# Second half of the attention: order of casts, scores and MLP steps, and a residual added by DMA

## The chip, the cores and the metric

The kernel runs on one core of a Trainium2 chip. The metric is the device time of one execution in microseconds (us). Every time in this document is of that one core; the profile shows TensorE as PE (matmuls) and PEld (weight loads), VectorE as DVE, ScalarE as ACT, GpSimd as POOL, and SyncE, which only issues DMAs here, as SP.

## The reference, cut to what matters

A two-layer trunk on 1024 tokens of width 1024, in float32. Layer 0 mixes with a matrix memory, layer 1 with causal attention over a shared low-rank key and value; each mixer is followed by an MLP with squared ReLU. The change lies in layer 1:

```
def causal_mla_attention(q_nope, q_rope, k_nope, k_rope, v):    # 8 heads, blocks of 128 queries
    s = (einsum('bqhd,bkhd->bhqk', qn_b, k_nope)
         + einsum('bqhd,bkd->bhqk', qr_b, k_rope)).astype(float32) * scale
    s = where(kpos[None, :] <= qpos[:, None], s, -inf)
    p = softmax(s, axis=-1)
    return einsum('bhqk,bkhd->bqhd', p.astype(v.dtype), v)

# layer 1
y = mla_mixer(h, ...)                          # attention, then @ w_out
x = x + g1[:, None, :] * rmsnorm(y, norm_g[l, 1])          # "the residual" of this document
h = modulate(rmsnorm(x, norm_g[l, 2]), sh2, sc2)
y = square(relu(h @ w1)) @ w2
x = x + g2[:, None, :] * rmsnorm(y, norm_g[l, 3])
```

## The kernel before, in words

The tokens are worked on in two halves of 512. A float32 product is made of three matmuls on a high and a low part of each operand (`mm3`, L280 to L282), so every weight and every activation is split first: a cast on ACT makes the high part, a subtraction on DVE the low part (`wsplit`, L238 and L239, for weights; `split_mod`, L501 and L502, for activations).

Two streams of work are woven by hand in `two_streams`. The *other* stream is what has to go on in order: here `mixer1` of the second half, that is its key and query latents, its attention (`attention_second`, `attend_beside`), the output projection `wout` and `post`. The *dense* stream is an MLP: here layer 1's MLP on the first half (`sweep1`), whose products need nothing from the second half. The other stream yields numbers. A number is how many dense steps are put into TensorE's order at that place; a 0 forgets what was still due. In `sweep1` each step consists of two pieces that count a half, and each piece is 12 matmuls of 512 columns: a hidden step (`first`: TensorE writes `ps`) or an up step (`up_rows`: TensorE writes `pm` and DVE adds it to the sums, L247). "align" runs the dense stream on until a hidden step is next. The order of TensorE's instructions is thereby written out; on the other engines a scheduler orders what is ready by priority. Work inside `prompt` has high priority: the weight loads with their splits, the softmax, and the evacuations. `tc.issue_after(i)` puts what is issued in its block behind instruction `i` on `i`'s engine; `paced()` uses it to put parts of `residual` and `post` behind the last DVE instruction of the dense piece before. An MLP weight is loaded and split two steps ahead of its products (`AHEAD`). `sweep1` has 64 pieces; behind them comes `sweep2`, the same MLP on the second half, and it needs what `post` makes.

`attend_beside` goes through 16 units: 8 heads, each with 256 queries `j` = 2 (6 key blocks) and then 256 queries `j` = 3 (8 key blocks). A unit has two scores `e` = 0, 1 of 128 queries each; a score is up to 1024 columns wide. `softmax_two` takes it from PSUM: maximum (DVE L1824), two exponentials (ACT L1826), sum and reciprocal (DVE L1829, L1830), two scalings (DVE L1832). For `e` = 0 the probabilities lie in a tile `raw`, shared with the weight loads, for `e` = 1 in two tiles `tmc`. `turned` transposes four blocks on TensorE (L2031) and splits them; `products` multiplies the values with blocks turned two rounds before. Per unit, in TensorE's order: for each pair of key blocks its transposes, then products, and in the first two rounds behind these a score of the *next* unit (`then`); at the unit's end `yield next(dense)`.

`post` calls `residual`: the sum of squares of `y` is made on ACT (L484) and DVE (L488), TensorE sums it over the partitions (L492), a short chain gives the factor, eight DVE instructions scale `y` (L956), eight add the old `x` (L959) that SP has loaded from `xs` (L926), and SP stores each block to `xs` (L962). Then the same begins again on the new `x`: squares, sums, L492. ACT also scales `y` in place (L2701) and DVE makes differences of it (L2702) for the MLP's second half; their results go through L2715 to L2733. `WAITS` are the dense steps put between: ahead of the first sum, after the first and second four blocks, ahead of the second sum.

The lines that set these numbers:

```
        yield from attend_beside(hf, units(), cycle((0.5, 0.5, 0)), lambda: load_o(hf))
...
    WAITS = (2, 1, 0.5, 3, 0, 0)
```

Of the kernel before, what the change touches and what calls it, by code (L numbers as in the profile page):

```python
# [9 lines left out]
F32 = mybir.dt.float32  # L10
# [4 lines left out]
ALU = mybir.AluOpType  # L15
AX = mybir.AxisListType

P = 128
D = 1024
S = 1024  # L20
H = 512
# [61 lines left out]
def kernel(  # L83
# [27 lines left out]
    nc = tc.nc  # L111
# [4 lines left out]
    ts = lambda i, n: slice(i * n, (i + 1) * n)  # L116
# [45 lines left out]
    def scratch(shape, name):  # L162
        return dr.tile(shape, F32, tag=name, bufs=1, name=name)
# [62 lines left out]
    class Half:  # L226
        pass

    pace, follow = [None], [False]

    def paced():

        return tc.issue_after(pace[0]) if pace[0] else nullcontext()

    def wsplit(r, n):
        hi = sb.tile([P, 1024], F32R, tag="ws", bufs=WS, name=f"wh_{next(uid)}")
        lo = sb.tile([P, 1024], F32R, tag="ws", bufs=WS, name=f"wl_{next(uid)}")
        nc.scalar.copy(hi[:, :n], r[:, :n])  # L238
        i = nc.vector.tensor_sub(lo[:, :n], r[:, :n], hi[:, :n].bitcast(F32))  # L239
        if follow[0]:  # L240
            pace[0] = i.ins
        return hi, lo
# [169 lines left out]
    SH1, SC1, G1, SH2, SC2, G2 = range(6)  # L412
    adac = lambda l, part: ada[:, l, ts(part, 8)]
# [60 lines left out]
    def rstd_steps(blocks, n):  # L474

        accs = []
        for b in blocks:
            square_to(accs, b)
        yield
        return sums_rstd(accs[0], n, tmc())  # L480
# [439 lines left out]
    xs = scratch([D, S], "xs")  # L920
    xs_blk = lambda k, half: xs[ts(k, P), ts(half, H)]
# [22 lines left out]

    def residual(y, half, B, src, first, each=None, n3=1, n7=1):

        blk = src(half)
        yield 0
        rs = rstd_steps([y[k] for k in range(KD)], D)
        next(rs)  # L950
        yield first
        rstd = last_of(rs)
        yield 0
        for k in range(KD):
            with paced():
                nc.vector.scalar_tensor_tensor(  # L956
                    y[k], y[k], B[:, k : k + 1], rstd, ALU.mult, ALU.mult
                )
                nc.vector.tensor_add(y[k], y[k], blk(k))  # L959
                if each:  # L960
                    each(k)
            nc.sync.dma_start(xs_blk(k, half), y[k])  # L962
            if k % 4 == 3:
                yield n7 if k == KD - 1 else n3

# [854 lines left out]
    def softmax_two(f, pr, n):  # L1820


        m, l, a = small(1), small(1), small(2)
        nc.vector.reduce_max(m, f[:, :n], axis=AX.X, negate=True)  # L1824
        for g, w in ((0, 512), (1, n - 512)):
            nc.scalar.activation(  # L1826
                pr[g][:, :w], f[:, g * 512 : g * 512 + w], AF.Exp, bias=m, accum_out=a[:, g : g + 1]
            )
        nc.vector.tensor_add(l, a[:, 0:1], a[:, 1:2])  # L1829
        nc.vector.reciprocal(l, l)  # L1830
        for g, w in ((0, 512), (1, n - 512)):
            nc.vector.tensor_scalar(pr[g][:, :w], pr[g][:, :w], l, None, ALU.mult)  # L1832

    def softmax(f, pr, n):
        m, l = small(1), small(1)
# [183 lines left out]
    def attend_beside(hf, units, dense, behind):  # L2019

        def turned(u, b):
            t = hdv(F32R)
            pt = pc()
            turns = [(0, b), (1, b), (0, b + 1), (1, b + 1)]
            if b + 2 == u.nk:
                turns.pop(2)
            for m, (i, kb) in enumerate(turns):  # L2030
                nc.tensor.transpose(  # L2031
                    pt[:, ts(m, P)], u.prs[i][kb // 4][:, ts(kb % 4, P)], ident
                )
            w = len(turns) * P
            split_mod(t[:, 0, :w], t[:, 1, :w], pt[:, :w], None)
            return t

        def products(u, b, t):
            if b == 0:
                u.po = ps()[:, :256]  # L2040
            for kb in (b, b + 1):
                last = kb == u.nk - 1
                o = u.po[:, P:] if last else u.po
                at = slice((kb - b) * 256, (kb - b) * 256 + (P if last else 256))
                mm3(o, *u.v[kb], t[:, 0, at], t[:, 1, at], kb == 0, last)
            if b + 2 == u.nk:
                s = ts(u.j % 2, 256)
                if u.hh < 6:
                    o = tmp()[:, :256]
                    nc.scalar.copy(o, u.po)  # L2050
                    nc.sync.dma_start(oT[ts(u.hh, P), ts(u.j, 256)], o)
                else:
                    split_mod(hf.o.hi[u.hh][:, s], hf.o.lo[u.hh][:, s], u.po, None)

        def unit():
            g = next(units, None)
            if g is None:
                return None
            u = Half()
            (u.hh, u.q, u.kn, u.v), u.j = g  # L2060
            u.nk, u.prs = 2 * u.j + 2, []
            return u

        def score(u, e):
            i = 2 * u.j + e
            st = pm()
            score_two(st, hf.kk, u.q, u.kn, i)
            if e:
                pr = [tmc(), tmc()]
            else:  # L2070
                pr = raw()
                pr = [pr[:, 0:512], pr[:, 512:1024]]
            prompt(softmax_two)(st.rearrange("p a b -> p (a b)"), pr, (i + 1) * P)
            u.prs.append(pr)

        yield "align"
        u = unit()
        for e in range(2):
            score(u, e)
        yield 1  # L2080
        behind_, waiting = [behind], []
        while u:
            then = unit()
            for n, b in enumerate(range(0, u.nk, 2)):
                waiting.append((u, b, turned(u, b)))
                yield 0
                if len(waiting) > 2:
                    products(*waiting.pop(0))
                    yield 0
                if n < 2:  # L2090
                    if then:
                        score(then, n)
                        yield 0
                    elif behind_:
                        behind_.pop()()
            yield next(dense)
            u = then
        for w in waiting:
            products(*w)
# [99 lines left out]
    def attention_second(hf):  # L2199
        pairs = [prepare_pair(p_, hf) for p_ in range(4)]  # L2200
        next(pairs[0])
        yield 0
        for p_ in range(4):
            if p_ < 3:
                yield from primed(pairs[p_], pairs[p_ + 1])
            else:

                yield next(pairs[p_])
                first = loaded_head(0)
                yield from pairs[p_]  # L2210

        def units():
            for hh in range(NH):
                h_ = loaded_head(hh) if hh else first
                if hh == 6:
                    last_o(hf)
                for j in range(2, 4):
                    yield h_, j

        yield from attend_beside(hf, units(), cycle((0.5, 0.5, 0)), lambda: load_o(hf))  # L2220

    def primed(g, then):

# [13 lines left out]
    def load_o(hf):  # L2237
        o, half = hf.o, hf.i
        for b in range(3):
            o.hi.t[b], o.lo.t[b] = k4v(F32R), k4v(F32R)  # L2240
            r = raw().rearrange("p (a b) -> p a b", b=512)
            nc.sync.dma_start(
                r, oT[2 * b * P : (2 * b + 2) * P, ts(half, H)].rearrange("(k p) n -> p k n", p=P)
            )
            nc.scalar.copy(o.hi.t[b], r)
            nc.vector.tensor_sub(o.lo.t[b], r, o.hi.t[b].bitcast(F32))
# [225 lines left out]
    m = [pm(), pm()]  # L2472
# [11 lines left out]
    hf, h = hfs[0], Split()  # L2484
# [281 lines left out]
    ms = [Mlp(0, False), Mlp(1, True)]  # L2766
# [138 lines left out]
    def mixer1(hf, z, attention):  # L2905
        att = attention(hf)
        lat = latent(hf, lambda: next(att))
        next(lat)

        yield from to_x(hf, z)  # L2910
        yield from lat
        yield next(att)
        yield "fill"
        yield from att
        y = FH(claim=True)
        last = wout(b_w_out[0], hf.o, lambda m, pt: evac(y[m], pt), ahead=2 - 2 * hf.i)
        if not hf.i:
            next(last)
        yield 1
        yield "align"  # L2920
        for _ in last:
            yield 0
        yield 1
        if hf.i:
            yield from post(hf, y, B2, x_cols, A3, adac(1, SH2), ms[1], WAITS)
        else:
            yield from post_second(hf, y, B2, x_cols, A3, adac(1, SH2))

# [15 lines left out]
        mixer1(hfs[0], z0, attention_first), bg_rest(),  # L2944
    )

    WAITS = (2, 1, 0.5, 3, 0, 0)
    u0, u1, swept = FH(claim=True), Half(), [False]

    def aside():  # L2950
# [57 lines left out]
```

## Time and profile before

| | |
|---|---|
| median of 3 runs | 2339.51 us |
| lowest and highest of them | 2333.42 and 2341.66 us |
| the profiled execution | 2334.96 us |
| its span in the profile | 2333.2 us |
| PE busy | 2253.4 us, 97% |
| DVE busy | 1682.5 us, 72% |
| ACT busy | 1109.4 us, 48% |
| POOL busy | 137.0 us, 6% |

The span is 1.8 us shorter than the time of the same execution, and that execution is 4.6 us under the median. Overlapped matmuls make PE look full where it only follows its order; where PE does wait, the profile names what ended the wait. A row of the timeline gives the start, the duration, the engine, the line, the tile written and the tiles read; in brackets stands how long the engine had been idle and what it was released by. A row of a group gives count, busy time and mean. PEclk is the granted TensorE clock as a share of full speed.

### The profile page before, as it was taken

How to read it: one execution, taken by the hardware profiler on the slowest of the kernel's cores; microseconds unless marked ns; L12 is line 12 of the kernel's file. 1: busy time of each engine (PE TensorE's matmuls, PEld its weight loads, DVE VectorE, ACT ScalarE, POOL GpSimd, SP SyncE). 2: the span in 40 equal slices, each digit the busy share in tenths (PEclk: the TensorE clock that was granted, in tenths of full speed). 3: DMA queues.
4: the chain of work that ended last, by engine and by line, in shares of the span. 5: the costliest groups of instructions: out<-in, count | busy, mean ns of one | idle time of the engine just before them, and what ended most of it. 6: DMA issues, size and time to landing. Idle time of an engine off the chain costs nothing. (4 is left out here: it accounts for less than half of the span.)

```text
span 2333.2 us, 30865 instructions
## 1 busy us (share of the span) xinstructions
PE 2253.4 (97%) x11050; PEld 1861.1 (80%) x11050; DVE 1682.5 (72%) x2733; ACT 1109.4 (48%) x1925; POOL 137.0 (6%) x228
## 2 busy tenths in 40 slices
PE   8999999999999999999999999998897899999998
PEld 6888887888888878788888877787785688888887
DVE  6677767889887877777757678666638876765556
ACT  4365335865344455445445555444434333354433
POOL 1000000011122210000000000000000211100000
PEclk9999999999999999999999999999998899999999
DMA  9544554668999886677668656844335686666421
GB/s 318 190 122 125 162 155 144 212 215 279 341 293 293 283 302 211 217 220 223 226 193 279 226 177 230 288 142 173 115 96 190 197 258 219 212 215 207 161 90 64
DMA packets 400234, 482.01 MB, mean 207 GB/s; under 512 B 28788, under 2 KB 270513, under 8 KB 400081
## 3 DMA queue, kind: packets, MB, share of 16 engines
q1 hardware_dynamic: 381248, 413.87, 55.3%
q0 software_dynamic: 18832, 66.17, 7.7%
q8 instruction: 87, 1.43, 0.2%
q14 instruction: 67, 0.54, 0.1%
HBM read 358.33 MB, written 121.63 MB: 206 GB/s over the span
## 5 line engine op out<-in xcount | busy, mean ns | idle before, releaser
L238 ACT CAST wh<-raw 128x1024 fp32r<-128x1024 f32 (+4 forms) x301 | 305.1, 1015 | 416.7 <-PE ps L281 150.1
L239 DVE TENSOR_TENSOR wl<-raw,wh 128x1024 fp32r<-128x1024 f32 (+4 forms) x301 | 354.8, 1181 | 191.3 <-ACT wh L238 165.6
L280 PE MATMUL ps<-k,wh 128*128 128x512 f32 x1109 | 438.4, 395 | 4.0 <-ACT wh L238 2.4
L281 PE MATMUL ps<-k,wh 128*128 128x512 f32 x1109 | 433.3, 391 | 3.5 <-DVE k L502 3.5
L282 PE MATMUL ps<-k,wl 128*128 128x512 f32 x1109 | 433.1, 391 | 0.0
L280 PEld LDWEIGHTS ps<-k,wh 128*128 128x128 f32 x1109 | 208.5, 188 | 50.8 <-ACT wh L238 3.4
L281 PEld LDWEIGHTS ps<-k,wh 128*128 128x128 f32 x1109 | 208.7, 188 | 47.7 <-DVE k L502 5.1
L282 PEld LDWEIGHTS ps<-k,wl 128*128 128x128 f32 x1109 | 208.7, 188 | 43.8
L247 DVE TENSOR_TENSOR k<-k,pm 128x512 f32<-128x512 f32 (+1 forms) x194 | 156.6, 836 | 70.2 <-PE pm L282 70.0
L280 PE MATMUL pm<-wh,hd 128*128 128x512 f32 x488 | 195.2, 400 | 8.5 <-DVE k L247 7.7
L282 PE MATMUL pm<-wh,hd 128*128 128x512 f32 x488 | 191.8, 393 | 2.2 <-DVE hd L502 2.2
L281 PE MATMUL pm<-wl,hd 128*128 128x512 f32 x488 | 192.0, 393 | 0.0
L280 PEld LDWEIGHTS pm<-wh,hd 128*128 128x128 f32 x488 | 92.9, 190 | 29.8 <-issue 9.1
L282 PEld LDWEIGHTS pm<-wh,hd 128*128 128x128 f32 x488 | 92.6, 190 | 22.5 <-DVE hd L502 2.8
L281 PEld LDWEIGHTS pm<-wl,hd 128*128 128x128 f32 x488 | 92.7, 190 | 20.0 <-issue 1.2
L280 PE MATMUL pm<-hd,wk 128*128 128x512 f32 x256 | 101.7, 397 | 2.3 <-ACT hd L501 2.3
L281 PE MATMUL pm<-hd,wk 128*128 128x512 f32 x256 | 100.5, 393 | 0.3 <-DVE hd L502 0.2
L282 PE MATMUL pm<-hd,wk 128*128 128x512 f32 x256 | 100.2, 391 | 0.0
L281 PE MATMUL pm<-hd,wh 128*128 128x512 f32 x256 | 99.6, 390 | 0.2 <-DVE hd L502 0.2
L282 PE MATMUL pm<-hd,wl 128*128 128x512 f32 x256 | 99.7, 389 | 0.0
L280 PE MATMUL pm<-hd,wh 128*128 128x512 f32 x256 | 99.2, 390 | 0.1
L986 ACT ACTIVATE tmp<-tmp 128x512 f32<-128x512 f32 x80 | 50.4, 630 | 81.3 <-DVE tmp L247 70.3
(495 smaller groups left out, 4751.4 us busy)
## 6 DMA issues: line engine op xcount, KB each, us to landing
raw<-in_mlp_w_dram SPq DMA_DIRECT2D x160, 512.0 KB, 4.7
raw<-in_mlp_w_dram SPq DMA_DIRECT2D x128, 256.0 KB, 4.7
raw<-in_ada_w_dram SPq DMA_DIRECT2D x54, 512.0 KB, 4.6
raw<-in_a_w_in_dram SPq DMA_DIRECT2D x44, 512.0 KB, 3.9
lo<-wl POOLq DMA_DIRECT2D x32, 512.0 KB, 6.4
s<-k POOLq DMA_DIRECT2D x32, 512.0 KB, 4.1
u<-k POOLq DMA_DIRECT2D x32, 512.0 KB, 5.5
raw<-s SPq DMA_DIRECT2D x32, 512.0 KB, 4.7
```

What stands on the lines that cost most here:

```text
L238: nc.scalar.copy(hi[:, :n], r[:, :n])
L239: i = nc.vector.tensor_sub(lo[:, :n], r[:, :n], hi[:, :n].bitcast(F32))
L247: return f(*a, **k)
L280: nc.tensor.matmul(o, lh, rh, start=start, stop=False)
L281: nc.tensor.matmul(o, lh, rl, start=False, stop=False)
L282: pe_last[0] = nc.tensor.matmul(o, ll, rh, start=False, stop=stop)
L986: nc.scalar.activation(s, s, AF.Relu)
```

## The change

Six edits, five of them in the second half's attention and what follows it:

- `softened()`: a weight's cast and subtraction are issued behind the last exponential (ACT) and the last scaling (DVE) of the latest `softmax_two`. The list is emptied in the last unit.
- `turned`: the four transposes go first through the two blocks of `e` = 0, then through those of `e` = 1. Where they are written stays as it was.
- `attend_beside`: the next unit's score stands ahead of the round's transposes and products, where it stood behind them. In the last unit `load_o` moves in the same way.
- `cycle((0.5, 0))` for `cycle((0.5, 0.5, 0))`: a dense piece in each `j` = 2 unit, none in a `j` = 3 unit.
- `residual` without `src` (second half of layer 1): no loads of `xs` and no additions on DVE. Behind every second block POOL issues a DMA that adds 512 KB of `xs` into `y` in SBUF, and SP then stores the two blocks to `xs`.
- `WAITS` from (2, 1, 0.5, 3, 0, 0) to (2.5, 1.5, 1, 4, 0, 0).

```
+    def softened():
+
+        c = ExitStack()
+        for i in soft:
+            c.enter_context(tc.issue_after(i))
+        return c
 
     def wsplit(r, n):
...
-        nc.scalar.copy(hi[:, :n], r[:, :n])
-        i = nc.vector.tensor_sub(lo[:, :n], r[:, :n], hi[:, :n].bitcast(F32))
+        with softened():
+            nc.scalar.copy(hi[:, :n], r[:, :n])
+            i = nc.vector.tensor_sub(lo[:, :n], r[:, :n], hi[:, :n].bitcast(F32))
...
     def residual(y, half, B, src, first, each=None, n3=1, n7=1):
 
-        blk = src(half)
+        blk = src and src(half)
...
-                nc.vector.tensor_add(y[k], y[k], blk(k))
+                if blk:
+                    nc.vector.tensor_add(y[k], y[k], blk(k))
                 if each:
                     each(k)
-            nc.sync.dma_start(xs_blk(k, half), y[k])
+            if blk:
+                nc.sync.dma_start(xs_blk(k, half), y[k])
+            elif k % 2:
+                x = xs[(k - 1) * P : (k + 1) * P, ts(half, H)].rearrange("(k p) n -> p k n", p=P)
+                nc.gpsimd.dma_start(y.t[k // 2], x, accum_op=ALU.add)
+                nc.sync.dma_start(x, y.t[k // 2])
...
     def softmax_two(f, pr, n):
...
-            nc.vector.tensor_scalar(pr[g][:, :w], pr[g][:, :w], l, None, ALU.mult)
+            d = nc.vector.tensor_scalar(pr[g][:, :w], pr[g][:, :w], l, None, ALU.mult)
+        soft[:] = [e.ins, d.ins]
...
-            for m, (i, kb) in enumerate(turns):
+            for m, (i, kb) in sorted(enumerate(turns), key=lambda t: t[1]):
...
             for n, b in enumerate(range(0, u.nk, 2)):
+                if n < 2:
+                    if then:
+                        score(then, n)
+                        yield 0
+                    elif behind_:
+                        soft.clear()
+                        behind_.pop()()
                 waiting.append((u, b, turned(u, b)))
                 yield 0
                 if len(waiting) > 2:
                     products(*waiting.pop(0))
                     yield 0
-                if n < 2:
-                    if then:
-                        score(then, n)
-                        yield 0
-                    elif behind_:
-                        behind_.pop()()
...
-        yield from attend_beside(hf, units(), cycle((0.5, 0.5, 0)), lambda: load_o(hf))
+        yield from attend_beside(hf, units(), cycle((0.5, 0)), lambda: load_o(hf))
...
-            yield from post(hf, y, B2, x_cols, A3, adac(1, SH2), ms[1], WAITS)
+            yield from post(hf, y, B2, None, A3, adac(1, SH2), ms[1], WAITS)
...
-    WAITS = (2, 1, 0.5, 3, 0, 0)
+    WAITS = (2.5, 1.5, 1, 4, 0, 0)
```

More of the change, by code (lines that the diff above doesn't have):

```diff
@@ L227 @@
         pass
-    pace, follow = [None], [False]
+    pace, follow, soft = [None], [False], []
     def paced():
         return tc.issue_after(pace[0]) if pace[0] else nullcontext()
+    def softened():
[3 more added lines that the diff above has]
+        return c
     def wsplit(r, n):
@@ L1825, in softmax_two @@
         for g, w in ((0, 512), (1, n - 512)):
-            nc.scalar.activation(
+            e = nc.scalar.activation(
                 pr[g][:, :w], f[:, g * 512 : g * 512 + w], AF.Exp, bias=m, accum_out=a[:, g : g + 1]
```

## The prediction, made before the changed kernel ran

> **What bounds the kernel now.** I read the page's head, then busy time and granted clock by stretch, then who waits for whom on PE, then the timeline at the waits.
>
> ```profile
> PE 2253.4 (97%) x11050; PEld 1861.1 (80%) x11050; DVE 1682.5 (72%) x2733; ACT 1109.4 (48%) x1925; POOL 137.0 (6%) x228
> ...
> core 0: us, PE busy (x) PEld busy (x) DVE busy (x) ACT busy (x) POOL busy (x), PEclk, DMA share, GB/s
> 1498.00:1680.00 182.00, 160.29 (x990) 138.60 (x989) 119.74 (x237) 88.56 (x213) 1.40 (x4) 0.97 0.42 146
> 1680.00:1751.00 71.00, 71.00 (x321) 58.99 (x320) 27.57 (x34) 27.31 (x38) 1.75 (x5) 1.00 0.37 111
> 1751.00:1850.00 99.00, 74.41 (x285) 57.00 (x284) 86.79 (x132) 41.63 (x65) 10.18 (x10) 0.84 0.55 179
> ```
>
> PE bounds the kernel: it lacks 80 us (2333.2 - 2253.4). Of these, 21.7 us lie in the attention (1498 to 1680) and 24.6 us in what follows the projection (1751 to 1850); between them PE is full. The clock column adds 0.03 x 182 = 5.5 us in the attention. In the last stretch 0.16 x 99 = 16 us looks larger, but much of it falls on idle time.
>
> ```profile
> PE pc L2031 <- DVE tmc L1832: 17.9, 8, 3.2
> PE pc L2031 <- DVE hd L502: 2.2, 2, 1.3
> ...
> PE pc L492 <- DVE tmc L488: 11.2, 1, 11.2
> PE pm L280 <- DVE k L247: 7.7, 2, 7.5
> ```
>
> In the attention PE waits for the scaled probabilities of `e` = 1; after it, for the squares of the second sum, then for DVE to take up an up step. One attention wait in time:
>
> ```profile
> 1641.14 0.48 PE L1818 MATMUL pm<-k,k 128*128 128x512 f32 x1
> 1641.93 1.22 DVE L1824 TENSOR_REDUCE sm<-pm 128x1 f32<-128x1024 f32 x1
> 1644.03 1.05 ACT L238 CAST wh<-raw 128x1024 fp32r<-128x1024 f32 x1 [1.51 <-DMA raw<-in_mlp_w_dram]
> 1644.98 0.68 ACT L1826 ACTIVATE tmc<-pm,sm 128x512 f32<-128x512 f32 x1
> 1645.11 1.22 DVE L239 TENSOR_TENSOR wl<-raw,wh 128x1024 fp32r<-128x1024 f32 x1 [1.50 <-ACT wh L238]
> 1646.25 1.28 DVE L247 TENSOR_TENSOR k<-k,pm 128x512 f32<-128x512 f32 x2
> 1647.45 0.15 DVE L1829 TENSOR_TENSOR sm<-sm 128x1 f32<-128x1 f32 x1
> 1647.83 0.88 DVE L1832 TENSOR_SCALAR tmc<-tmc,sm 128x512 f32<-128x512 f32 x2
> 1648.38 0.33 PE L2031 MATMUL pc<-ident,tmc 128*128 128x128 f32 x1 [2.85 <-DVE tmc L1832]
> ...
> 1652.64 0.43 PE L2031 MATMUL pc<-ident,raw 128*128 128x128 f32 x1
> 1653.87 0.45 PE L1812 MATMUL pm<-k,k 128*128 128x512 f32 x1
> 1655.80 0.27 PE L2031 MATMUL pc<-ident,raw 128*128 128x128 f32 x1
> ```
>
> The score ends at 1641.6, its probabilities at 1648.7: 7.1 us. The maximum is there at 1643.15, yet the exponential starts at 1644.98, behind a weight's cast that stood in ACT's queue waiting for its DMA. The last three rows: a round of transposes and products takes PE 1.2 us, a score of 768 columns 1.9 us.
>
> **The change part by part.**
>
> *Casts behind the softmax.* They leave 1.8 us of this chain (1643.15 to 1644.98) and the cast's DVE half, 1.14 us to the next start. Undisturbed the chain is 1.22 + two exponentials (1644.98 to 1646.43, 1.45) + 0.4 of small ones + 0.88, with 0.3 to start: 4.3 us for 1024 columns, less for fewer. Behind a held cast the splits of other tiles could queue, but its own releasers run just before it on its own queue. The weight waits too; it is needed two dense steps later, with a piece in every second unit that is eight units, half of the attention. If that cover failed PE would wait for cast and subtraction, 2.3 us each.
>
> *Transposes of `e` = 0 first.* Two of 0.11 us slip under each wait: between 0 and 8 x 0.2 us, taken as 0.
>
> *Scores ahead.* Nothing is added; score `e` = 1 comes one round earlier, and the next unit's score `e` = 0 now stands between a unit's end and the transposes that need `e` = 1. *Fewer steps* takes the piece out of the `j` = 3 units.
>
> ```profile
> L280 PE MATMUL pm<-wh,hd 128*128 128x512 f32 x24 | 9.5, 397 | 0.8 <-ACT raw L1826 0.8
> L280 PE MATMUL ps<-k,wh 128*128 128x512 f32 x19 | 7.5, 392 | 0.0
> ...
> 1757.47 0.39 PE L280 MATMUL ps<-k,wh 128*128 128x512 f32 x1
> 1762.91 0.39 PE L280 MATMUL pm<-wh,hd 128*128 128x512 f32 x1
> ```
>
> One of the three matmuls of a product stands four times in a piece: 24 and 19 (one record missing) are 11 pieces, as the cycle gives; two take 5.44 us, so one 2.72. Eight remain. Distance from the end of score `e` = 1 to the transposes that need it: before, 1.2 or 2.4 us of rounds plus 2.7 where there is a piece. After, for a 1024-column score (begun in a `j` = 2 unit) two rounds 2.4 + piece 2.7 + next score (640 columns, a little under the 1.9) 1.7 = 6.8; for a 768-column one three rounds 3.6 + next score 1.9 = 5.5. Against 4.3 this leaves 2.5 and 1.2 us, room for three or two splits of 0.7 us (0.72 each for L488 below, of the same kind and size). I take 4 of 21.7 us as left (the drain of the last unit, 2.2 us on L502, has no next score): **-17.5**, bounds -20 and -8 (half). With the waits goes the cold clock, **-4.5** of 5.5. The three pieces taken out are 8.2 us of PE work done later, no gain in themselves. Nor is the lighter attention bound by DVE: 119.7 less three pieces of 1.5 us (below) in a stretch of about 152 (182 - 17.5 - 4.5 - 8.2).
>
> Row, then rule:
>
> ```profile
> 1511.56 0.33 PE L2031 MATMUL pc<-ident,tmc 128*128 128x128 f32 x1 [1.92 <-DVE tmc L1832]
> ...
> 1510.00:1520.00 10.00, 8.44 (x50) 7.75 (x51) 5.63 (x14) 2.77 (x8) 0.00 (x0) 0.83 0.05 16
> ```
>
> A wait of 1.92 us stands beside a clock of 0.83. The Trainium skill, TensorE: Matmul & The Clock Gate, Part 1, has the clock halve after about one idle window of 3.4 us. By that no attention wait (longest 3.2) would cost clock, and the sum would be 4.5 us smaller; the trace disagrees.
>
> *Ahead of the projection.* The pieces of `mixer1` up to there add up to 39 before (10 + 5 + 8, 1 to align, 2, 11, 2) and 36 after; 39 needs one more to reach a hidden step, 36 none. So one piece fewer between attention and projection, and none in the last unit: 5.4 us less cover for `load_o` and the first projection weights on SP, ACT and DVE. 0 to 5.4, taken **+1.5**.
>
> *Residual by DMA, and more steps after.*
>
> ```profile
> 1751.13 1.02 PE L492 MATMUL pc<-tmc,ones 128*128 128x512 f32 x2
> 1788.59 2.08 PE L492 MATMUL pc<-tmc,ones 128*128 128x512 f32 x2 [11.25 <-DVE tmc L488]
> 1791.74 0.63 PE L280 MATMUL pm<-wh,hd 128*128 128x512 f32 x1
> 1812.90 0.76 PE L280 MATMUL pm<-wh,hd 128*128 128x512 f32 x1 [7.48 <-DVE k L247]
> ...
> 1760.61 5.39 DVE L956 SCALAR_TENSOR_TENSOR k<-k,mods,tmc 128x512 f32<-128x512 f32 x8
> 1765.91 1.29 DVE L959 TENSOR_TENSOR k<-k,tmc 128x512 f32<-128x512 f32 x2
> 1785.67 2.87 DVE L488 TENSOR_TENSOR tmc<-tmc,tmc 128x512 f32<-128x512 f32 x4
> 1781.85 0.72 ACT L2701 ACTIVATE k<-k,mods 128x512 f32<-128x512 f32 x1 [1.49 <-DMA xs<-k]
> ...
> lo<-wl POOLq DMA_DIRECT2D x32, 512.0 KB, 6.4
> u<-k POOLq DMA_DIRECT2D x32, 512.0 KB, 5.5
> k<-xs SPq DMA_DIRECT2D x8, 512.0 KB, 10.5
> ```
>
> From the first sum (T = 0) to the second are 9 pieces, 24.5 us, then PE waits 11.25. After: 2 x (1.5 + 1 + 4) = 13 pieces, 0.5 + 35.4 us; the fifth piece ahead of T = 0 is mere work, nothing waits there. Is the second sum ready by T + 36? The last scaling ends at T + 14.9 (1766.0); the second four now stand behind the DVE work of three pieces, due by T + 12, so that holds. The eight additions, 0.6 us each to the next start, 4.9 us of DVE, go, with eight loads and four of eight stores on SP. In their place POOL issues four accumulates. No row shows one; the nearest are POOL's 512 KB, 5.5 and 6.4 us to landing, and 512 KB from `xs`, 10.5; read twice, an estimated 21 at worst, 4 at best. I take 8: landed T + 23.5, last square and sum T + 25.5. Even 18 fits. The stores follow, each holding SP until its accumulate has landed; behind them stand weight loads, used two steps (10.9 us) later. L2701 waits for the stores, as it does now by 1.49 us, but is needed only after the second sum. DVE is the tighter cover: 13 pieces (an up step is four L247 of 0.6 and an L239 of 1.14, 3.6; a hidden step L247, L502 and L239, 2.4; 3.5 of the one and 3 of the other, 19.5, so 1.5 a piece) + chain 2.8 + scalings 5.4 + seven sums 4.3 + four differences 2.4 = 34.4 of 36 us (0.6 each; the chain is four instructions of 0.7). So 1.5 us of the wait stays: **-9.7**, bounds -11.2 and, with accumulates of 21 us ending at T + 38 and a full DVE behind, -5. The cold start behind it goes: L492 took 2.08 us for 1.02, and matmuls behind it 0.63 for 0.39, some five of them 0.2 us longer to the next start: **-2**. Behind the second sum 8 of the 64 pieces are left for 9 before (36 + 2 + 5 + 13 done for 40 + 2 + 4 + 9); DVE sets that stretch and loses one piece's 1.5 us while PE loses 2.7 of cover: **+1**; the 7.48 us wait stays.
>
> **Sum:** -17.5 - 4.5 + 1.5 - 9.7 - 2 + 1 = -31.2 on the profiled 2334.96: 2304. That execution is 4.6 us under the median 2339.51; on the median it is 2308. I say 2307.
>
> Against accumulates speaks this: the Trainium skill, SBUF — State Buffer, Who interferes with whom, says that descriptor generation on GpSimd is blocked while DVE is in its two-port modes. What it would do here is a rival below.
>
> ```profile
> 1761.27 0.54 POOL L1015 DMA_DIRECT2D m<-tmp  x1 [11.24 <-ACT tmp L251]
> ```
>
> In the middle of L956, with DVE full, POOL issues a DMA in 0.54 us. By that rule the trace shows no blocking from these instructions.
>
> **The rivals.** (1) *Half of the attention's waits stay*, moved to another tile: for it, DVE and ACT are shared by two softmaxes, splits and up steps; against it, the 1.2 us of room or more. 2307 + 10 = 2317. (2) *The second sum still waits*: accumulates issue late, each held by POOL until DVE pauses (the page named last, as a mechanism here), or land after T + 36. The 11 us stay: 2318. (3) *Nothing*: casts and pieces only change places and DVE, 86.8 of 99 us after the projection, gives all of it back: 2338. For it, DVE's fullness there; against it, the attention's idle DVE. (4) *Slower, by SP.* The stores stand in SP's queue ahead of weight loads. If the four accumulates took 21 us each, one behind the other, the last would land at T + 15.5 + 84 = T + 99.5, 64 us after PE has run out of pieces: 2307 + 64 = 2371. It decides from T + 36 + 31 = T + 67, 13 us each in series; against it, 10.5 us is the slowest such row, and DMAs overlap.
>
> **How the numbers follow.** Forecast 0.60 (its own range 2299 to 2315), rival 1 0.13, rival 2 0.10 (0.03 of it late issue), rival 3 0.08, rival 4 0.06, more than forecast 0.03. Before's runs spread by 0.35%, so 0.3%, 7 us, is about what can be told: faster is under 2332.5. The first, rivals 1 and 2 and the last make 0.86; because several effects may join I give 0.80 faster, 0.11 same, 0.09 slower. The range from 2297 to 2330 leaves out rivals 3, 4 and a little of the forecast.
>
> **What would show it.** Right: the waits of L2031 for L1832 under 3 us together, no weight cast between L1824 and L1826, clock 0.99 in the attention, the second L492 waiting under 3 us, accumulates landing within 10. Wrong: new PE waits for weights (L238, L239), for `hd` in the attention, L492 still waiting for L488, SP idle on an accumulate with weight loads behind.

## The result, and the profile after

The changed kernel took 2314.82 us (median of 4 runs, 2313.02 to 2318.59), the kernel before 2339.68 us on the same chip (4 runs, 2333.42 to 2341.66): a ratio of 0.990 with a 95% interval from 0.9878 to 0.9923. A second measurement on another chip gave 0.9906 (0.989 to 0.9923). The profiled execution took 2313.79 us, its span is 2312.0 us, 21.2 us under that of before.

The page's head, and busy time and clock by stretch (columns as in the prediction; the stretches end earlier than before, since the kernel is ahead of its old times):

```profile
PE 2249.8 (97%) x11050; PEld 1860.4 (80%) x11050; DVE 1679.0 (73%) x2725; ACT 1109.5 (48%) x1925; POOL 142.8 (6%) x232
```

```profile
1498.00:1650.00 152.00, 145.80 (x951) 128.92 (x950) 115.82 (x232) 86.78 (x211) 1.81 (x5) 1.00 0.51 176
1650.00:1723.00 73.00, 73.00 (x332) 61.24 (x331) 27.65 (x35) 27.55 (x39) 1.28 (x4) 0.98 0.33 100
1723.00:1830.00 107.00, 85.28 (x321) 65.98 (x320) 88.30 (x132) 43.17 (x67) 17.19 (x15) 0.86 0.59 174
```

PE's idle time fell from 79.8 us to 62.2 (2312.0 - 2249.8), by 17.6; its busy time fell by 3.6, which is clock, since it executes the same 11050 matmuls. The attention now takes 152 us where it took 182, with three pieces less in it, and its clock is 1.00.

Who waits for whom on PE, first in the attention and then from the first sum on:

```profile
PE pc L2046 <- DVE hd L510: 4.9, 1, 4.9
PE ps L288 <- DVE k L510: 1.3, 1, 1.3
...
PE pm L288 <- DVE k L255: 10.3, 2, 8.0
PE pm L288 <- ACT hd L509: 3.3, 1, 3.3
PE ps L289 <- DVE k L510: 3.0, 3, 1.8
PE pc L2274 <- DMA tmc<-xs: 2.8, 1, 2.8
PE ps L288 <- ACT wv L1056: 1.3, 1, 1.3
PE ps L290 <- DVE wv L1057: 1.0, 1, 1.0
```

All lines lie further down than before: the transposes of the attention are L2046 (L2031), the mm3 lines L288 to L290 (L280 to L282), the sum over the partitions L500 (L492), its squares L492 and L496 (L484, L488), an up step's addition L255 (L247), a split L509 and L510 (L501, L502), a weight's L246 and L247 (L238, L239), the scalings of the softmax L1846 (L1832). The 17.9 us for the scaled probabilities and the 11.2 us for the squares are gone. Three things stand in their place: 4.9 us at the attention's end, 3.3 us for ACT, and more waiting behind the second sum: without the 3.3 us the last six rows give 18.4 us, where before had 13.4 (24.6 - 11.2). In all: attention 21.7 to 6.2, from the first sum on 24.6 to 21.7. Together that is 18.4 us less waiting (elsewhere PE's idle time grew by 0.8), of which 15.5 us are the attention's: most of the gain, though not all of it.

### The profile page after: what moved, and what is told of

The parts are those of the page before. It is cut to its first block, busy times and chain, and to the rows that moved or that the text cites. A ratio compares the mean times of both kernels' runs of the same rounds, so it can differ in the third digit from the quotient of the medians.

```text
span 2312.0 us, 30830 instructions
## 1 busy us (share of the span) xinstructions
PE 2249.8 (97%) x11050; PEld 1860.4 (80%) x11050; DVE 1679.0 (73%) x2725; ACT 1109.5 (48%) x1925; POOL 142.8 (6%) x232
## 4 chain that ended last, share of the span: by engine, by line
PE 78%; DVE 8%; DMA 8%; issue 3%; ACT 2%; POOL 0%; SPq 0%; DVEq 0%; ACTq 0%; POOLq 0%
PE ps L288 13%; PE ps L289 13%; PE ps L290 13%; PE pm L289 8%; PE pm L288 8%; PE pm L290 8%; DMA raw<-in_mlp_w_dram 3%; PE pc L288 1%; PE pc L289 1%; PE pc L290 1%; DVE k L255 1%; PE pc L2046 1%; DVE wl L247 1%; DMA s<-k 1%; DMA raw<-s 1%
## 5 line engine op out<-in xcount | busy, mean ns | idle before, releaser
L246 ACT CAST wh<-raw 128x1024 fp32r<-128x1024 f32 (+4 forms) x301 | 304.8, 1014 | 397.5 <-PE ps L289 148.0
L247 DVE TENSOR_TENSOR wl<-raw,wh 128x1024 fp32r<-128x1024 f32 (+4 forms) x301 | 355.6, 1183 | 190.0 <-ACT wh L246 163.7
L288 PE MATMUL ps<-k,wh 128*128 128x512 f32 x1109 | 438.6, 395 | 5.4 <-DVE k L510 2.5
L290 PE MATMUL ps<-k,wl 128*128 128x512 f32 x1109 | 432.8, 390 | 0.0
L288 PEld LDWEIGHTS ps<-k,wh 128*128 128x128 f32 x1109 | 208.4, 188 | 52.7 <-ACT wh L246 3.4
L290 PEld LDWEIGHTS ps<-k,wl 128*128 128x128 f32 x1109 | 208.5, 188 | 43.7
L288 PE MATMUL pm<-wh,hd 128*128 128x512 f32 x488 | 194.7, 399 | 13.6 <-DVE k L255 10.3
L255 DVE TENSOR_TENSOR k<-k,pm 128x512 f32<-128x512 f32 (+1 forms) x194 | 156.6, 838 | 69.2 <-PE pm L290 69.1
L290 PE MATMUL pm<-wh,hd 128*128 128x512 f32 x488 | 192.2, 394 | 0.0
L288 PEld LDWEIGHTS pm<-wh,hd 128*128 128x128 f32 x488 | 93.1, 191 | 34.4 <-issue 9.1
L290 PEld LDWEIGHTS pm<-wh,hd 128*128 128x128 f32 x488 | 93.0, 191 | 20.0 <-DVE hd L510 0.3
L288 PE MATMUL pm<-hd,wk 128*128 128x512 f32 x256 | 101.3, 396 | 2.5 <-ACT hd L509 2.5
L290 PE MATMUL pm<-hd,wk 128*128 128x512 f32 x256 | 99.7, 389 | 0.0
L290 PE MATMUL pm<-hd,wl 128*128 128x512 f32 x256 | 99.6, 389 | 0.0
L288 PE MATMUL pm<-hd,wh 128*128 128x512 f32 x256 | 99.3, 390 | 0.2 <-ACT hd L509 0.2
L1000 ACT ACTIVATE tmp<-tmp 128x512 f32<-128x512 f32 x80 | 50.5, 631 | 92.0 <-DVE tmp L255 80.7
```

Source lines behind the costliest of these rows:

```text
L255: return f(*a, **k)
L288: nc.tensor.matmul(o, lh, rh, start=start, stop=False)
L290: pe_last[0] = nc.tensor.matmul(o, ll, rh, start=False, stop=stop)
L1000: nc.scalar.activation(s, s, AF.Relu)
```

## The experiments

The theory after this reading: the attention's edits bring the whole gain, and the edits behind the projection (residual by DMA, larger `WAITS`) only move a wait from ahead of the second sum to behind it, since DVE is full there. The rivals: each part brings what the sum gave it; or it is one edit alone, and the others are idle. Ratios are to the kernel before, on the same chip in the same series; the brackets hold the 95% interval.

**The attention alone.** The kernel before with casts behind the softmax, scores ahead, transposes reordered and the new cycle; the additions and `WAITS` as they were. Against the changed kernel:

```
-            yield from post(hf, y, B2, None, A3, adac(1, SH2), ms[1], WAITS)
+            yield from post(hf, y, B2, x_cols, A3, adac(1, SH2), ms[1], WAITS)
...
-    WAITS = (2.5, 1.5, 1, 4, 0, 0)
+    WAITS = (2, 1, 0.5, 3, 0, 0)
```

> The kernel before with the attention edits alone (casts, scores, transposes, cycle), the residual by loads and additions and the old WAITS. Theory A (the whole gain is the attention's; pieces moved ahead of the second sum are missing behind it, and the accumulates land too late to help): the attention waits fall from 22 to 6 us, the second sum waits 11 us as before, the waits behind it fall from 13 to 5 us or so because four pieces more are left for that stretch, 0.986 to 0.990 of before, no slower than the changed kernel. Rival D (the DMA residual and the new WAITS carry 8 us or more of the gain): 0.993 to 0.996.

Measured: 2310.14 us, 0.9897 (0.9877 to 0.9917). The changed kernel itself ran beside it once more:

> The changed kernel itself, unchanged, beside the three others of this job, so that their times have a neighbour on the same chip. Every theory: 0.990 of the kernel before, 0.988 to 0.992.

Measured: 2313.46 us, 0.9906 (0.989 to 0.9923). The attention's edits alone give as much as the whole change. The waits of PE from the first sum on, with the attention's edits alone:

```profile
PE pc L500 <- DVE tmc L496: 11.6, 1, 11.6
PE pc L2274 <- DMA tmc<-xs: 8.6, 3, 3.2
PE ps L289 <- DVE k L510: 1.9, 3, 0.9
PE pm L288 <- DVE k L255: 0.8, 1, 0.8
```

The wait ahead of the second sum is there (11.6 us), but behind it there are 11.3 us, not 18.4: 22.9 us in all against the changed kernel's 21.7.

**The edits behind the projection alone.** Residual by DMA, new `WAITS`, reordered transposes; the attention's other edits undone (the list `soft` never filled, the block with the score moved back behind the products, `cycle((0.5, 0.5, 0))`).

> The kernel before with the other half alone: residual by DMA and the new WAITS (and the order of the four transposes), attention as before. Theory A (pieces between the sums are taken from behind the second sum): the attention's waits stay near 22 us, the second sum no longer waits, but 60 of 64 pieces are then used for 55 before, so the waits behind it grow from 13 to some 25 us; 0.997 to 1.003 of before. Rival D (the post's edits are a gain of their own, 8 us or more): 0.993 to 0.996.

Measured: 2342.7 us, 1.0041 (1.0025 to 1.0056): slower. Its waits of PE in the attention, and from the first sum on:

```profile
PE pc L2045 <- DVE tmc L1846: 17.3, 8, 3.3
...
PE ps L288 <- ACT wv L1056: 24.7, 1, 24.7
PE pc L500 <- DVE tmc L496: 4.7, 1, 4.7
```

With the pieces of the old cycle kept in the attention and 13 more ahead of the second sum, 60 of the 64 pieces are used when the sum comes (the prediction's count, 40 + 2 + 5 + 13). Four remain for a stretch in which DVE makes the input of `sweep2`, and PE stands still for 24.7 us ahead of the first hidden step of `sweep2`. In the 20 us from 1810 to 1830, inside this wait, DVE is busy all the time.

**The changed kernel with the old cycle** isolates this:

```
-        yield from attend_beside(hf, units(), cycle((0.5, 0)), lambda: load_o(hf))
+        yield from attend_beside(hf, units(), cycle((0.5, 0.5, 0)), lambda: load_o(hf))
```

> The changed kernel with the old cycle: 11 pieces in the attention. Theory A (distance suffices either way; the three or four pieces are missing behind the second sum): waits for the scalings stay under 3 us, the waits behind the second sum grow from 18 to 23 us or more, 3 to 8 us slower than the changed kernel, 0.992 to 0.994 of before. Rival H (pieces in the attention are as good as anywhere): within 2 us of the changed kernel, 0.990.

Measured: 2322.95 us, 0.9958 (0.9944 to 0.9972), some 0.5% (12 us) behind the changed kernel in its other series, more than the 3 to 8 us that were expected. One row of its waits tells it:

```profile
PE ps L288 <- ACT wv L1056: 25.3, 1, 25.3
```

The 60 pieces return, and the same wait with them. The attention of this kernel has only two waits of 1.3 us together for L1846, so the pieces that the new cycle takes out are not missed there and are wanted later. Beside the new `WAITS` the new cycle is thus a part of the gain that the prediction called "no gain in themselves"; what it does beside the old ones, no run shows.

**Casts and distance.** Three kernels take the two edits of the attention apart, all with the new cycle and the new end. Casts free: the line `soft[:] = [e.ins, d.ins]` left out. Scores behind: the block `if n < 2: ...` stands behind the products again. Neither: both undone.

> The changed kernel (2314.8 us) with one edit undone: weight casts may again be issued ahead of a softmax. Theory A (the casts were part of each late chain: 7.1 us with a cast in it, 4.3 without, against 6.8 and 5.5 us of distance): a dense weight is split in about four of the sixteen units, so three to five waits of L2031 of 0.3 to 1.6 us come back, 3 to 5 us in all, 2318 to 2321. Rival B (the larger distance alone removed the waits): no wait of L2031 for the scalings comes back, 2314 to 2316.

> The changed kernel with the scores again behind the round's transposes and products, casts still behind the softmax. Theory A (distance and casts both count): the distances fall to 1.2 + 2.7 = 3.9 us in the units with a piece and 2.4 us in those without, against chains of 4.3 us and a little less, so waits of about 0.4 and 1.5 us in turn, some 15 us in the attention, 2328 to 2332. Rival C (the casts alone made the chain late): under 3 us of waits, 2315 to 2318.

> The changed kernel with both attention orders undone, casts free and scores behind; the new cycle stays. It stands against the run that only has the scores behind (9.4 us of waits for the scalings, 0.997). Theory A (a cast in the chain costs 1.8 to 2.9 us, in four of the sixteen units): 4 to 8 us more waits, 0.999 to 1.001. Rival B (casts cost nothing, only distance counts): waits of 9 to 10 us again, 0.997.

Measured: casts free 2315.29 us, scores behind 2325.61 us, neither 2335.43 us. The table has the ratios, with those of the changed kernel in its first row.

| | casts behind the softmax | casts free |
|---|---|---|
| scores ahead | 0.990 (0.9878 to 0.9923), 0.9906 (0.989 to 0.9923) | 0.9925 (0.9904 to 0.9947) |
| scores behind | 0.9972 (0.9959 to 0.9985) | 1.0012 (1.0001 to 1.0024) |

The waits of PE for the scaled probabilities with casts free, with scores behind, and with neither:

```profile
PE pc L2045 <- DVE tmc L1846: 1.1, 1, 1.1
```

```profile
PE pc L2046 <- DVE tmc L1846: 9.4, 9, 1.9
```

```profile
PE pc L2045 <- DVE tmc L1846: 18.1, 12, 3.7
```

With short distance a free cast costs 8.7 us (18.1 against 9.4), 0.4% by the table (1.0012 to 0.9972, intervals apart). With the scores ahead it costs 1.1 us in one wait, and the times (0.9925 against 0.990 and 0.9906, intervals overlapping) do not tell it from nothing. So distance does nearly all of it alone, and the casts' edit would take half of the waits if it stood alone. The two are not additive, as the prediction's chain (a shorter chain and a longer cover for the same wait) implies. "Neither" differs from the edits behind the projection alone (1.0041, 1.0025 to 1.0056) in nothing but the new cycle, which is worth 0.3% there too (intervals apart).

**The residual and the `WAITS`.** First the additions in place of the DMA, with the new `WAITS` (`x_cols` for `None` in the call of `post`); then the DMA with the old `WAITS`, `(2, 1, 0.5, 3, 0, 0)`:

> The changed kernel with the residual as it was before: x loaded by SP and added on DVE, stores of single blocks; the new WAITS stay. Theory A (the accumulate and its store, 9.5 and 9.3 us to landing, cost as much as the 4.9 us of DVE that they save: ACT waits 6.9 us for a store in front of a hidden step's ReLU): the PE wait of 3.3 us for ACT goes, a wait of 0 to 5 us for the squares (L492 for L488 in the lines of before) comes, 2312 to 2318. Rival D (the DMA residual is what removed the wait for the second sum): that wait comes back with 5 to 10 us, 2320 to 2326.

> The changed kernel with the old WAITS (9 pieces between the two sums and 4 ahead of the first, where it has 13 and 5). Theory A (pieces moved ahead of the second sum are missing behind it, where PE now waits 18 us for DVE): the second sum waits 8 to 12 us, the waits behind it fall from 18 to 10 or 12 us because five more pieces are there, net 0 to 6 us slower, 2315 to 2321. Rival E (the pieces between the sums are pure gain): the second sum waits 8 to 12 us and the waits behind stay at 18, 2323 to 2328.

Measured: with additions 2311.72 us, 0.9915 (0.99 to 0.993); with the old `WAITS` 2303.2 us, 0.9876 (0.986 to 0.9891). The first is level with the changed kernel: the wait for the squares returns with 6.9 us, but the 3.3 us for ACT go and the longest wait for L255 shrinks from 8.0 to 5.4. The second went against what was expected: its ratio is below the changed kernel's 0.990 and 0.9906, though the intervals still touch (a kernel below, with the same `WAITS` and in one series with the changed kernel, has them apart). Its waits of PE from the first sum on:

```profile
PE pc L500 <- DVE tmc L496: 10.1, 1, 10.1
PE pc L2274 <- DMA tmc<-xs: 8.0, 3, 2.8
PE pm L288 <- DVE k L255: 0.8, 1, 0.8
PE ps L289 <- DVE k L510: 0.4, 2, 0.2
```

The second sum waits 10.1 us again, and behind it 9.2 us are left of 18.4. With 51 pieces used (36 + 2 + 4 + 9) 13 remain for the stretch that DVE bounds. By waits this is 19.3 us for 21.7. The two spans (2312.0 and 2300.3) differ by more, 11.7 us, but the first transposes of this attention, up to which the two programs are alike, already lie 5.2 us apart, in the changed kernel and here:

```profile
1502.15 0.38 PE L2046 MATMUL pc<-ident,raw 128*128 128x128 f32 x2
```

```profile
1496.96 0.38 PE L2046 MATMUL pc<-ident,raw 128*128 128x128 f32 x2
```

That part is no effect of the `WAITS`. Of the 6.5 us from there on, the waits are 2.4 and the clock is some of the rest (0.91 for 0.89 from 1723 to 1860, 0.02 x 137 = 2.7 us); what remains, about 1 us, stays open.

**Is it ACT's queue?** In the changed kernel ACT stands for 6.86 us on a store ahead of L2717, and a hidden step's ReLU stands behind it (rows below). So the scalings L2717 and their differences were issued behind ACT's work of the next three dense steps:

```
+            if src:
+                scale()
+            else:
+                yield waits[3] - 1
+                act = next(i for i in reversed(nc.cur_bb.bb.instructions) if i.engine == act_eng)
+                with tc.issue_after(act):
+                    scale()
-        yield waits[3]
+        yield waits[3] if src or not hf.i else 1
```

> The changed kernel with the in-place scaling of the new x on ACT, and its differences on DVE, issued behind ACT's work of the next three dense steps, so that they no longer stand with their wait for the stores (6.9 us) ahead of a hidden step's ReLU. Theory A (ACT's queue held by a store is what made PE wait 3.3 us ahead of the second sum): that wait goes, the second sum is ready some 5 us earlier, and the differences still come in time, 3 to 5 us faster than the changed kernel. Rival F (DVE sets the stretch, the 3.3 us only come back behind the second sum): the wait goes and the ones behind grow, within 1 us of the changed kernel.

Here `scale()` makes the eight L2717 and the four L2718. Measured: 2312.51 us, 0.99 (0.9883 to 0.9918), level with the changed kernel. Its waits of PE from the first sum on, and its two sums:

```profile
PE pm L288 <- DVE k L255: 14.9, 4, 6.6
PE ps L289 <- DVE k L510: 2.6, 4, 1.9
PE ps L288 <- ACT wv L1056: 1.4, 1, 1.4
PE ps L290 <- DVE wv L1057: 1.0, 1, 1.0
...
1726.37 1.02 PE L500 MATMUL pc<-tmc,ones 128*128 128x512 f32 x2
1762.63 1.02 PE L500 MATMUL pc<-tmc,ones 128*128 128x512 f32 x2
```

The 3.3 us for ACT are gone, and the second sum starts 36.3 us after the first (1762.63 - 1726.37), without a wait, where the changed kernel needs 41.4: ACT's queue is what held it up. Behind it the waits for DVE's L255 rose from 10.3 to 14.9, so that the rows make 19.9 us for 18.4, and a part of what was won comes back in the stretch that DVE fills. Something seems left: from the first sum to the end of the span this execution took 586.0 us (2312.4 - 1726.37), the changed kernel 589.2 (2312.0 - 1722.78). The medians, 2312.51 and 2313.46, don't tell that from nothing.

**A better version.** The old `WAITS`, and at the attention's end the list is set to the splits of the last unit's transposes in place of being emptied, so that the casts of later weights stay behind these:

```
-            split_mod(t[:, 0, :w], t[:, 1, :w], pt[:, :w], None)
+            e = nc.scalar.copy(t[:, 0, :w], pt[:, :w])
+            d = nc.vector.tensor_sub(t[:, 1, :w], pt[:, :w], t[:, 0, :w].bitcast(F32))
+            if (u.hh, u.j) == (NH - 1, 3):
+                soft[:] = [e.ins, d.ins]
...
-                        soft.clear()
```

> The changed kernel with the old WAITS, and in the last unit of the attention the weight casts are held behind the splits of the transposed blocks, where the change lets them go free. Theory A (the 4.9 us wait of the last transposes comes from casts of MLP and projection weights that stand in ACT's queue, waiting for their DMAs, ahead of those splits): that wait falls under 1 us and the projection does not wait for its weights, 5 to 6 us below the kernel with the old WAITS alone, 0.985 of before. Rival G (without the cover the projection waits for its weights instead): the wait goes over to L288 for L246 or L247, 0 to 2 us gained.

Measured: 2300.69 us, 0.9855 (0.9835 to 0.9875), beside 2313.46 us for the changed kernel in the same series. The wait at the attention's end:

```profile
PE pc L2046 <- DVE hd L2051: 3.1, 1, 3.1
```

It fell from 4.9 to 3.1 us, not under 1 us as expected: the casts held up 1.8 us of it. What makes up the rest is not shown; on ACT a hidden step's ReLU (L1000), which waits 2.23 us for DVE, still stands ahead of the last splits. No wait of the projection for its weights came in its place. Last, the same kernel with the twelve late DVE instructions of `post` (L2747 to L2749 of the changed kernel) issued behind those that the first transposes of the MLP's input need:

```
-                nc.vector.scalar_tensor_tensor(
+                behind_u = nc.vector.scalar_tensor_tensor(
...
+            with tc.issue_after(behind_u.ins):
+                nc.vector.tensor_mul(y[k], y[k], rstd)
+                nc.vector.tensor_sub(y[k], y[k], u[k])
+                nc.vector.tensor_mul(y[4 + k], y[4 + k], rstd)
```

> The kernel with old WAITS and casts held to the attention's end, and besides, the twelve DVE instructions of post that are needed last (7.2 us, lines L2747 to L2749 of the changed kernel) issued behind those needed first. Theory A (DVE sets the stretch behind the second sum, and these twelve stand in it too early): the waits there, 8.5 us in the run without this edit, fall by 3 to 6 us, 0.983 of before. Rival I (what PE waits for there is loads and other DVE work): 0 to 1 us, 0.9855.

Measured: 2302.07 us, 0.9868 (0.9852 to 0.9883), no gain over the one before: the wait for `xs` falls (3.4 to 2.2 us), the one for L255 rises (4.3 to 5.3). The three kernels with the DMA and the old `WAITS` are at 2300.69, 2302.07 and 2303.2 us; their intervals overlap, so which of them is best isn't settled. All three have a lower ratio than the changed kernel; for the first (0.9835 to 0.9875 beside 0.989 to 0.9923 in the same series) the intervals are apart, for the other two they still touch the changed kernel's. Nor is it settled what the DMA is worth in them: with the additions and the old `WAITS` the ratio was 0.9897 (0.9877 to 0.9917), with the DMA 0.9876 (0.986 to 0.9891), on different chips and overlapping.

## Why the prediction came out as it did

The forecast was 2307 us on a median of 2339.51, a gain of 32.5; measured were 24.9 us (2339.68 - 2314.82), and 20.7 in the second series (2334.12 - 2313.46). The time lies inside the range of 2297 to 2330, but it is at the end of the forecast's own 2299 to 2315 and near rivals 1 and 2 (2317 and 2318): the time alone can't tell these apart, the waits can, and that the shortfall still fitted the range was luck. The mechanism of the attention was right, and the loss against the forecast lies almost wholly behind the projection, where the steps named below failed.

**The attention's waits: -17.5, found -15.5.** The waits for the scaled probabilities have all gone. But at the attention's end PE waits 6.2 us, where 4 were allowed, 2.2 of them for the drain: 1.28 us at 1639.50 for a split, and 4.92 us in the drain:

```profile
1643.04 1.05 ACT L246 CAST wh<-raw 128x1024 fp32r<-128x1024 f32 x1 [1.40 <-DMA raw<-in_mlp_w_dram]
1646.02 1.04 ACT L246 CAST wh<-raw 128x1024 fp32r<-128x1024 f32 x1 [0.33 <-DMA raw<-in_b_w_out_dram]
1647.49 1.06 ACT L509 CAST hd<-pc 128x512 fp32r<-128x512 f32 x2
...
1649.67 0.66 PE L2046 MATMUL pc<-ident,raw 128*128 128x128 f32 x2 [4.92 <-DVE hd L510]
```

The list of the new rule is emptied in the last unit. Its casts then stand on ACT ahead of the last splits, each behind its DMA: the very wait that the edit removes elsewhere. The prediction had the "new PE waits for `hd` in the attention" among what would go wrong, without this place. *Ahead of the projection, +1.5*: no wait stands between 1649.67 and the first sum at 1722.78, so the cover was enough and the term is 0.

**The clock: -4.5 and -2, found -3.6 together.** In the attention the column went from 0.97 to 1.00 (0.03 x 182 = 5.5 us of such time before), but in the row behind it from 1.00 to 0.98 (0.02 x 73 = 1.5 us), after the wait in the drain. Some 4 us are left, so that term holds. The Trainium skill, TensorE: Matmul & The Clock Gate, Part 1, with its idle window of 3.4 us, would have put none of it down to waits of 3.2 us and less; the clock rose as these waits went, which speaks against the window as a lower limit. Single waits of up to 1.9 us are not enough, though: the kernel with the scores behind, with nine of them, has a clock of 1.00, the one with neither edit, with waits of up to 3.7 us, longer than the window, 0.97 (from 1498 to 1665, one row of each):

```profile
1498.00:1665.00 167.00, 154.04 (x985) 133.10 (x984) 117.46 (x234) 88.30 (x213) 1.53 (x6) 1.00 0.48 163
```

```profile
1498.00:1665.00 167.00, 148.94 (x922) 128.67 (x921) 107.72 (x218) 79.35 (x199) 1.58 (x5) 0.97 0.40 145
```

The row of 1.92 us beside 0.83 in the prediction is thus no proof that so short a wait is enough; what else acts there stays open. From the first sum on little came back: 0.86 where it was 0.84, over stretches of unlike length, since the waits behind the second sum grew.

**The second sum: -9.7, found -7.9.** The wait of 11.25 us went, and 3.31 us for ACT came; the row of the second sum has no bracket:

```profile
1722.78 1.02 PE L500 MATMUL pc<-tmc,ones 128*128 128x512 f32 x2
1758.43 0.69 PE L288 MATMUL pm<-wh,hd 128*128 128x512 f32 x1 [3.31 <-ACT hd L509]
1764.21 1.02 PE L500 MATMUL pc<-tmc,ones 128*128 128x512 f32 x2
1784.13 0.76 PE L288 MATMUL pm<-wh,hd 128*128 128x512 f32 x1 [7.97 <-DVE k L255]
1795.46 0.66 PE L2274 MATMUL pc<-ident,tmc 128*128 128x128 f32 x4 [2.76 <-DMA tmc<-xs]
```

It went for another reason than the one given. "Landed T + 23.5, last square and sum T + 25.5" was wrong by far: PE's sum starts at T + 41.4 (1764.21 - 1722.78), and the last square is made just ahead of it:

```profile
1763.29 0.69 DVE L496 TENSOR_TENSOR tmc<-tmc,tmc 128x512 f32<-128x512 f32 x1
```

Before, it started at T + 37.5 (1788.59 - 1751.13; the prediction's 24.5 and 11.25 make only 35.8, since PE spent 1.7 us more on the way than its nine pieces). So the four further pieces moved PE's arrival by some 11 us and ACT's hold by 3.3 more, and the sum became ready some 4 us later, not earlier. With the old cycle, where PE is not held by ACT, it comes before the squares are there and waits 4.7 and 4.9 us (the runs above with 60 pieces). The steps that failed are in these rows of the source views of the accumulates and of the stores, and of POOL, SP and ACT:

```profile
DMA to landing us min/median/max: 6.1/9.5/11.7
```

```profile
DMA to landing us min/median/max: 5.4/9.3/12.1
```

```profile
1733.18 2.52 POOL L975 DMA_DIRECT2D k<-xs  x2 [2.44 <-DVE k L964]
1739.31 1.18 POOL L975 DMA_DIRECT2D k<-xs  x1 [3.61 <-issue]
1745.55 0.60 POOL L1029 DMA_DIRECT2D m<-tmp  x1 [5.05 <-ACT tmp L259]
1746.14 1.23 POOL L975 DMA_DIRECT2D k<-xs  x1
...
1751.07 5.26 SPq L976 DMA_DIRECT2D xs<-k  x1
...
1739.26 1.16 ACT L492 ACTIVATE tmc<-k 128x512 f32<-128x512 f32 x2 [2.74 <-DMA k<-xs]
1743.62 1.15 ACT L492 ACTIVATE tmc<-k 128x512 f32<-128x512 f32 x2 [2.26 <-DMA k<-xs]
1755.88 1.33 ACT L2717 ACTIVATE k<-k,mods 128x512 f32<-128x512 f32 x2 [6.86 <-DMA xs<-k]
1757.12 0.61 ACT L1001 ACTIVATE tmp<-tmp 128x512 f32<-128x512 f32 x1
```

The last accumulate is issued at 1746.14, T + 23.4, where T + 15.5 was assumed. The last scaling ends at 1741.3 (1740.56 + 0.76, a row L964), T + 18.5, itself 3.6 us later than the T + 14.9 that the prediction kept from before; and in POOL's queue a DMA of the dense stream (L1029) stood ahead of it and waited 5.05 us for ACT. And an accumulate takes up to 11.7 us to land, not 8. The size of 8 was near (median 9.5), the start was not. Then ACT, whose rows follow one another in its queue's order, waits twice for an accumulate (2.74 and 2.26 us) and 6.86 us for a store of `xs`. The prediction said that L2701 (now L2717) "is needed only after the second sum". The instruction is, but behind it in ACT's queue stands the ReLU of a hidden step (L1001), then the split of what it makes, and PE waits 3.31 us for that split. With that hold taken out, in the run with the late scaling, the sum does come at the forecast's T + 36. It was the prediction's own question (what is queued behind the waiting instruction), answered for SP and neither for ACT nor for POOL.

**Behind the second sum: +1, found +5.0.** This is the term that was mis-sized most: 13.4 us of waits became 18.4, though only one piece fewer is left. The wait of 7.48 us that "stays" is 7.97, and 10.4 us follow it. A window of the changed kernel shows the cause:

```profile
1764.00:1785.00 21.00, 13.03 (x54) 10.19 (x53) 20.93 (x33) 9.33 (x16) 0.58 (x1) 0.86 0.36 118
```

DVE is busy for 20.93 of 21 us while PE works for 13. What is on DVE there (the split of the weight, the up steps' sums, the differences L2718, which are late as their scalings waited for the store, and the instructions of the MLP's input, L2731 to L2749) has to pass whatever PE does. A piece put ahead of the second sum is a piece less of cover for this stretch. The prediction counted the pieces that it moved forward as a gain of 2.7 us each and the ones missing later by a difference of one. The runs with 51, 56 and 60 pieces used show the exchange: 9.2, 18.4 and 30.8 us of waits behind the sum (30.8 = 25.3 + 5.1 + 0.4), against 10.1, 0 (3.3 for ACT) and 4.9 ahead of it.

**The rivals.** Rival 1 (half of the attention's waits stay) fell. Rival 2 (the second sum still waits) fell by its wait, but accumulates were late, as it said; what held the last one on POOL was a DMA that waited for ACT, and no lack of a pause on DVE. Rival 3 (DVE gives it back behind the projection) is right for the edits behind the projection, which it priced too widely by adding the attention's. Rival 4 (SP) did not come: one store held SP for 5.26 us with weight loads behind it, and up to the second sum no wait of PE goes back to them.

## What to carry to other kernels

Filler work that runs beside two waits is one sum: before moving it ahead of the first wait, count what remains for the second, and look there for the engine that is full. To hide a chain of other engines, first issue its start earlier in the order of the engine that waits; keeping other work out of the chain's way then adds little, though it helps by itself where the distance can't be had. For every wait that a change adds, list what stands behind it in that engine's queue, and for every rule that keeps work back, the place where the rule ends.

## What was not expected of the hardware

An accumulating DMA of 512 KB costs POOL 1.18 to 1.25 us to issue, where plain ones of the same size took 0.53 to 0.58, and a busy DVE does not change it: at 1733.18 two of them take 2.52 us while DVE has hardly a gap, and at 1746.14, with DVE idle, one takes 1.23. The Trainium skill, SBUF — State Buffer, Who interferes with whom, has GpSimd's descriptor generation blocked in DVE's two-port modes, but it names copies, casts and `tensor_scalar` as the instructions that can enter them and says that `tensor_tensor` has none. The DVE instructions beside these issues, and beside the row at 1761.27 in the prediction, are TENSOR_TENSOR and SCALAR_TENSOR_TENSOR, so neither row is a test of that rule. The stores of `xs` right behind the accumulates took 9.3 us to landing (median), where the stores of before, over the whole kernel, 256 KB each and without accumulates beside them, took 4.4.
